# A chunked delta rule: the state updates of two heads as one full-height matmul, from values spread over zero-padded tiles

## The chip, the core and the metric

The kernel runs on one core of a Trainium2 chip. The core has a matrix engine (TensorE, called PE in profiles; its weight loads are listed apart as PEld), a vector engine (VectorE, DVE), an activation engine (ScalarE, ACT), GpSimd (POOL) and a queue that mostly issues transfers (SyncE, SP). Data lies in SBUF, matmul results in the eight banks of PSUM, the rest in HBM. Both on-chip memories have 128 partitions; "height" below is the number of partitions that an instruction works on. The metric is the device time of one execution in microseconds, the median of several runs.

## What is computed

One step of a two-layer streaming encoder for 2048 new frames of one stream and 32 frames of a running one, in fp32. The first layer is sliding-window attention, the second a gated delta rule with 8 heads, keys and values 128 wide, in chunks of 64 frames. The change lies in the second. Its recurrence, cut to what matters:

```python
def step(s, xs):                      # one chunk of 64 frames, all heads
    qi, ki, ui, wi, gi, ai = xs
    v_new = ui - einsum('bhcd,bhde->bhce', wi, s)
    o = einsum('bhcd,bhde->bhce', qi * exp(gi)[..., None], s) + einsum('bhij,bhje->bhie', ai, v_new)
    g_last = gi[..., -1]
    s = s * exp(g_last)[..., None, None] + einsum(
        'bhcd,bhce->bhde', ki * exp(g_last[..., None] - gi)[..., None], v_new)
    return s, o
```

The state `s` is 128x128 for each head. The last line is the state update that the change touches: for each head the transposed, weighted keys (64 frames x 128) times the new values (64 frames x 128).

## The kernel before

The 2048 frames run in four slabs of 512 (the second carries the 32 frames of the other stream too). For each slab the first layer's projections and attention are done, all four slabs first, then the second layer slab by slab. A slab of the second layer has 33 input blocks, each a product of 1024x128 weights with the slab (24 matmuls into a bank `pj`, each 512 or 272 columns wide, in a reduced fp32 format `fp32r`, high and low parts apart), and 8 output blocks. Beside these blocks run generators ("sides"): convolution, gates, the inverse of the chunk's triangular matrix, and the chain that walks through the chunks.

Heads go in pairs. The 64 frames of a chunk for the first head of the pair lie on partitions 0 to 63, those of the second on 64 to 127, so that one 128-partition tile holds both. Four chunks form a quad, and `chain_quad` (from line 1617) walks through its four chunks in order, since each needs the state left by the one before. There are 33 quads (4 slabs x 4 pairs x 2, and one for the other stream), so 132 steps. Quads of index 0 and 1 have buffers of their own, so that a quad of one pair can run beside a quad of the next pair. One step is:

1. two matmuls of keys and queries (`kq`) with the two heads' states (`st`), into a PSUM bank `tb` (p1);
2. `r` on DVE (two instructions of 64 partitions) and `qs` on ACT (two of 64), from p1;
3. a matmul of the inverse (`tt`, in profiles `btt`) with `r`, into a second bank `tb` (p2): the new values of both heads, one below the other;
4. an ACT copy of them into `vn`, 128x128;
5. the state updates: for each head the 64 rows of `kd` (weighted keys) as weights, and the 64 rows of `vn`, give a 128x128 product. The first head's goes to the bank `tc` (p3), the second's to a free quarter of p2, because two such matmuls on different halves of the rows go to different banks;
6. a matmul of `it` (in profiles `bit`, the masked products of queries and keys) with `vn`, into p2;
7. on DVE one instruction for each head, state = state x decay + product (`st<-st,egl,tc` and `st<-st,egl,tb`), and the sum `o`;
8. on ACT the squares of `o`.

The program is written once by generators and then sorted: `Order` (line 211) keeps all recorded operations with their dependencies, and `flush` places them engine by engine with the planner's costs (`Estimate.cost`, line 119), the operations of a step ahead of others (`lead = Order.CHAIN`). A PSUM bank counts as a whole in these dependencies: a DVE read of p2 is placed after every PE write to p2 that was recorded before it. Each engine then runs its list in order. For PE, the planner's cost of a 128x128 fp32 matmul and its cost of one 128x256 wide are nearly in the ratio 1 to 2.

All the instructions issued through this layer bear line 185 in the profile, so the tiles' names tell them apart: `tc<-vn,kd` and `tb<-vn,kd` are the two updates, `tb<-vn,bit` the matmul of point 6.

Of the kernel before, what the change touches and what calls it, by code (L numbers as in the profile page):

```python
# [16 lines left out]
P = 128  # L17
# [5 lines left out]
CH = 64  # L23
# [359 lines left out]
class Kern:  # L383
# [846 lines left out]
    def delta_setup(self, bp):  # L1230
        nc = self.nc
        self.bp = bp
        one = lambda shape, tag, dt=F32: self.t(bp, shape, tag, dt, bufs=1)
        self.st = one([P, DNH, P], "st")
        self.hist = one([P, 24, 3], "hist")
        nc.gpsimd.memset(self.hist, 0.0)
        self.hsmp = one([P, 24, 3], "hsmp")
        nc.sync.dma_start(self.hsmp, self.io["cv"])
        self.csmp = one([P, 24, 3], "csmp")

        self.cw = one([P, 96], "cw")
        nc.vector.tensor_scalar(out=self.cw, in0=self.par[:, PC_CW : PC_CW + 96], scalar1=0.5, scalar2=None, op0=ALU.mult)
        self.dg = one([P, 1], "dgn")
        nc.vector.tensor_scalar(out=self.dg, in0=self.par[:, PC_DG : PC_DG + 1], scalar1=0.5, scalar2=None, op0=ALU.mult)
        self.na_ = one([P, 4], "na")
        nc.scalar.activation(self.na_, self.par[:, PC_AL : PC_AL + 4], AF.Exp)
        nc.vector.tensor_scalar(out=self.na_, in0=self.na_, scalar1=-1.0, scalar2=None, op0=ALU.mult)

        self.tts = [one([P, 4, P], f"btt{i}") for i in range(2)]
        self.its = [one([P, 4, P], f"bit{i}") for i in range(4)]  # L1250

        def zeros():
            for x in (*self.its, *self.tts, self.st):
                nc.gpsimd.memset(x, 0.0)
                yield 1000

        self.spawn(zeros(), "zeros", 5000)
        self.npair = self.nconv = 0
        self.chained, self.order, self.quads, self.had = set(), [], [], [None, None]
# [357 lines left out]
    def chain_quad(self, q, tab, off, states, gated, put):  # L1617


        nc, bp, m = self.nc, self.bp, 4  # L1620
        tt = nc.vector.tensor_tensor
        kq = q["kq"]
        yield from self.take(f"chain{q['i']}")
        yield from self.take("o", 2)
        o = self.t(bp, [P, 4, P], "o", bufs=2)
        so = self.t(bp, [P, 4], "so", bufs=2)
        al = q["al"]
        for c in range(m):
            state = yield from states(c)
            p1 = yield from self.bank("tb")  # L1630
            self.issue.lead = Order.CHAIN
            for x in range(2):
                self.mm(p1[:, x * P : (x + 1) * P], kq[:, c, x, :], state[:, x, :], True, True)
            r = self.t(bp, [P, P], f"r{q['i']}", bufs=1)
            qs = self.t(bp, [P, P], f"qs{q['i']}", bufs=1)
            half = [slice(y * CH, (y + 1) * CH) for y in range(2)]
            for x, rows in enumerate(half):
                nc.vector.scalar_tensor_tensor(
                    out=r[rows], in0=p1[rows, x * P : (x + 1) * P], scalar=q["nbk"][rows, c : c + 1], in1=q["vb"][rows, c, :],
                    op0=ALU.mult, op1=ALU.add)  # L1640
            for x, rows in enumerate(half[::-1]):
                nc.scalar.activation(
                    qs[rows], p1[rows, x * P : (x + 1) * P], AF.Identity, scale=tab["egq"][rows, off + c : off + c + 1])
            self.give("tb")
            self.issue.lead = 0
            yield
            p2 = yield from self.bank("tb")
            self.issue.lead = Order.CHAIN
            self.mm(p2[:, 0:P], q["tt"][:, c, :], r, True, True)
            vn = self.t(bp, [P, P], f"vn{q['i']}", bufs=1)  # L1650
            nc.scalar.copy(vn, p2[:, 0:P])
            self.issue.lead = 0
            yield

            p3 = yield from self.bank("tc")
            up = [p3[:, 0:P], p2[:, 2 * P : 3 * P]]
            self.issue.lead = Order.CHAIN
            for x in range(2):
                rows = slice(x * CH, (x + 1) * CH)
                self.mm(up[x], q["kd"][rows, c, :], vn[rows], True, True)  # L1660
            self.mm(p2[:, P : 2 * P], q["it"][:, c, :], vn, True, True)
            for x in range(2):
                nc.vector.scalar_tensor_tensor(
                    out=state[:, x, :], in0=state[:, x, :], scalar=tab["egl"][:, x, off + c : off + c + 1],
                    in1=up[x], op0=ALU.mult, op1=ALU.add)
            tt(out=o[:, c, :], in0=p2[:, P : 2 * P], in1=qs, op=ALU.add)
            self.issue.lead = 0
            self.give("tb")
            self.give("tc")
            yield  # L1670
            nc.scalar.activation(qs, o[:, c, :], AF.Square, accum_out=so[:, c : c + 1])
            states.done(c)

        q["over"].append("kq")
        self.give(f"chain{q['i']}")

        def rest():

            yield so
            tt(out=so[:, :m], in0=so[:, :m], in1=al, op=ALU.mult)  # L1680
            tt(out=so[:, :m], in0=so[:, :m], in1=al, op=ALU.mult)
            nc.vector.tensor_scalar(out=so[:, :m], in0=so[:, :m], scalar1=1.0 / P, scalar2=EPS, op0=ALU.mult, op1=ALU.add)
            nc.gpsimd.tensor_tensor(out=so[:, :m], in0=so[:, :m], in1=self.mhalf[:, :m], op=ALU.pow)
            yield
            tt(out=so[:, :m], in0=so[:, :m], in1=al, op=ALU.mult)
            yield
            for c in range(m):
                nc.scalar.activation(o[:, c, :], o[:, c, :], AF.Copy, scale=so[:, c : c + 1])
            yield
            po = yield from self.bank("ta")  # L1690
            for c in range(m):
                self.tp(po[:, c * P : (c + 1) * P], o[:, c, :])
            yield
            while not gated():
                yield 100
            zs = q["zs"]
            yield zs
            w = zs.shape[3]
            tt(out=zs, in0=po.rearrange("p (c x t) -> p c x t", x=2, t=CH)[:, :, :, :w], in1=zs, op=ALU.mult)
            self.give("ta")  # L1700
            self.give("o")
            yield
            yield from put(zs)
            q["over"].append("zs")

        return rest()
# [528 lines left out]
```

## Time and profile before

| | us |
|---|---|
| median of 3 runs | 2395.19 |
| lowest and highest | 2393.38, 2398.52 |
| the profiled execution | 2401.5 |
| its span, first to last instruction | 2399.7 |
| second layer in the span, from about | 1030 |

The mean granted TensorE clock of the profiled execution is 0.971 of full speed. In a profile's row of a group stand the line, the engine, the operation, the tiles (out<-in), the shape, the count, then busy time in us, the mean length of one in ns, and the idle time of the engine just before, with what ended it. Rows of the timeline begin with the start in us and the length; equal neighbours are merged, with their count at the end. A fp32 matmul of the program stands as two MATMUL records and two LDWEIGHTS records, so 132 matmuls count 264.

### The profile page before, as it was taken

What the parts mean: (1) busy time and instruction counts of PE and PEld (TensorE: products, weight loads), DVE (VectorE), ACT (ScalarE), POOL (GpSimd) and SP (SyncE); (2) the same over time, 40 slices, a digit from 0 to 9 for tenths busy, and PEclk for the clock granted to TensorE, in tenths of its full rate; (3) what the DMA queues carried; (4) which work ended last, traced back from release to release, by engine and by line L of the source; (5) the groups of instructions that cost most, each with busy time, mean ns of one, the idle gap of its engine ahead of it and who ended that gap; (6) DMA issues with size and microseconds to landing.
All of it is one profiled execution on the core that took longest, in us unless ns stands there. A gap on an engine that the chain in (4) does not pass through costs nothing.

```text
span 2399.7 us, 44456 instructions
## 1 busy us (share of the span) xinstructions
PE 2279.1 (95%) x14759; PEld 1851.9 (77%) x14759; DVE 1644.0 (69%) x5024; ACT 1265.6 (53%) x3792; POOL 864.4 (36%) x1044
## 2 busy tenths in 40 slices
PE   8999999899999999999999999999999999999997
PEld 5667888797778777777779798876798777777776
DVE  6765465726562546488888768888786888886876
ACT  5555465636553555355666454674554466445533
POOL 4566555565554333223322122331312222222222
PEclk9998999999999999999999999998999989999998
DMA  7565755476525124644334564334456634466541
GB/s 253 167 190 181 240 181 177 150 252 213 176 89 164 63 64 135 199 159 139 121 109 133 181 226 154 120 99 136 138 162 213 213 113 139 138 212 214 159 141 67
DMA packets 222832, 382.75 MB, mean 159 GB/s; under 512 B 29922, under 2 KB 45194, under 8 KB 222602
## 3 DMA queue, kind: packets, MB, share of 16 engines
q1 hardware_dynamic: 220154, 377.75, 49.4%
q8 instruction: 116, 1.90, 0.3%
q10 hardware_dynamic: 2448, 2.16, 0.3%
q14 instruction: 114, 0.93, 0.1%
HBM read 311.63 MB, written 68.19 MB: 158 GB/s over the span
## 4 chain that ended last, share of the span: by engine, by line
PE 57%; DVE 24%; ACT 7%; issue 3%; DMA 3%; POOL 2%; SPq 0%; DVEq 0%; ACTq 0%; POOLq 0%
PE pj L185 41%; PE tb L185 6%; PE ta L185 5%; PE tc L185 4%; DVE cy L185 3%; DVE s L185 3%; DVE sub L185 2%; DVE tl L185 2%; ACT s L185 1%; DVE ml L185 1%; ACT ta L185 1%; DVE r L185 1%; DVE mx L185 1%; DVE md L185 1%; DVE xa L185 1%
## 5 line engine op out<-in xcount | busy, mean ns | idle before, releaser
L185 PE MATMUL pj<-hk,wh 128*128 128x512 f32 (+1 forms) x8184 | 1796.7, 365 | 23.1 <-DVE xr L185 6.8
L185 PEld LDWEIGHTS pj<-hk,wh 128*128 128x128 f32 x8184 | 1331.4, 192 | 237.2 <-issue 22.9
L185 POOL TENSOR_TENSOR wh<-wr,wh 128x512 fp32r<-128x512 f32 x224 | 295.3, 1321 | 333.2 <-ACT wh L185 282.0
L185 DVE SCALAR_TENSOR_TENSOR cy<-cx,cw,cy 128x512 f32<-128x512 f32 x360 | 230.8, 651 | 45.0 <-ACT cy L185 40.3
L185 ACT CAST wh<-wr 128x512 fp32r<-128x512 f32 x224 | 137.7, 617 | 215.3 <-PE pj L185 164.3
L185 ACT ACTIVATE s<-s,mx 128x256 f32<-128x256 f32 (+1 forms) x272 | 132.0, 487 | 32.3 <-DVE mx L185 32.0
L185 ACT ACTIVATE qs<-tb,egq 64x128 f32<-64x128 f32 x264 | 95.8, 363 | 88.4 <-DVE r L185 76.0
L185 DVE TENSOR_SCALAR s<-s,den 128x256 f32<-128x256 f32 (+1 forms) x272 | 133.6, 542 | 1.3
L185 DVE TENSOR_TENSOR sub<-ml,tl 128x60 f32<-128x60 f32 (+24 forms) x527 | 126.5, 240 | 10.2
L185 ACT ACTIVATE cx<-cy 128x512 f32<-128x512 f32 (+1 forms) x96 | 61.1, 636 | 130.9 <-DVE cy L185 104.4
L185 DVE TENSOR_TENSOR tl<-tl,sub 128x60 f32<-128x60 f32 (+24 forms) x527 | 122.8, 233 | 10.0
L185 POOL TENSOR_TENSOR pr<-pr,ph 128x512 fp32r<-128x512 f32 x82 | 111.2, 1356 | 40.6 <-ACT ph L185 37.7
L185 DVE CUSTOM_DVE_ANT_0 s<-ta,bias 128x256 f32<-128x256 f32 (+1 forms) x272 | 96.3, 405 | 39.3 <-PE ta L185 38.0
L185 POOL COPY cx<-hist 128x3 f32<-128x3 f32 x96 | 26.7, 278 | 264.3 <-DVE kq L185 62.7
L185 DVE TENSOR_TENSOR xr<-pj,xr 128x512 f32<-128x512 f32 (+1 forms) x72 | 41.2, 577 | 108.3 <-PE pj L185 72.1
L185 POOL TENSOR_TENSOR so<-so,mhalf 128x4 f32<-128x4 f32 x33 | 36.8, 1114 | 218.0 <-DVE so L185 190.2
L185 DVE SCALAR_TENSOR_TENSOR r<-tb,nbk,vb 64x128 f32<-64x128 f32 x264 | 91.8, 348 | 29.9 <-PE tb L185 25.3
L185 ACT ACTIVATE qs<-o 128x128 f32<-128x128 f32 x132 | 40.7, 308 | 133.4 <-DVE o L185 128.1
L185 ACT COPY cx<-pj 128x512 f32<-128x512 f32 (+2 forms) x149 | 64.1, 446 | 78.9 <-PE pj L185 63.5
L185 PE MATMUL tc<-pt,vt 128*64 128x128 f32 (+2 forms) x1056 | 91.3, 289 | 12.1 <-ACT pt L185 11.3
L185 PE MATMUL tb<-st,kq 128*128 128x128 f32 x512 | 95.7, 289 | 6.4 <-DVE st L185 5.7
L185 PEld LDWEIGHTS tb<-st,kq 128*128 128x128 f32 x512 | 83.4, 196 | 21.3 <-DVE st L185 13.1
(242 smaller groups left out, 3578.6 us busy)
## 6 DMA issues: line engine op xcount, KB each, us to landing
wh<-xswwd SPq DMA_DIRECT2D x528, 256.0 KB, 2.9
wr<-in_wa SPq DMA_DIRECT2D x160, 256.0 KB, 2.9
wh<-xswwdo SPq DMA_DIRECT2D x112, 256.0 KB, 2.9
pr<-in_wd SPq DMA_DIRECT2D x66, 256.0 KB, 4.0
xswwd<-ph SPq DMA_DIRECT2D x66, 256.0 KB, 2.7
xswwd<-pr SPq DMA_DIRECT2D x66, 256.0 KB, 3.6
wr<-in_wao SPq DMA_DIRECT2D x64, 256.0 KB, 2.9
xa<-in_x SPq DMA_DIRECT2D x48, 256.0 KB, 3.3
```

The costliest lines, as they stand in the source:

```text
L185: self.order.add(Op(self.name, lambda: call(*args, **kw), cost, op == "dma_start"), ins, outs)
```

## The change

The new values are copied three times instead of once. Two copies of 64 partitions put the first head's values into the left half of a new tile `vz` (128 partitions x 2 x 128 values) and the second head's into its right half; the other rows of each half are zero, cleared once by GpSimd at the start of the layer. There are two such tiles, one for each quad index. Then one matmul with all 128 rows of `kd` as weights and all 256 columns of `vz` gives both heads' products, side by side in p3: the zero rows keep the heads apart. The third copy, of full height, fills `vn` as before, for the matmul with `it`. The quarter of p2 that held the second product is not used any more.

```diff
         self.its = [one([P, 4, P], f"bit{i}") for i in range(4)]
+        self.vz = [one([P, 2, P], f"vz{i}") for i in range(2)]
 
         def zeros():
-            for x in (*self.its, *self.tts, self.st):
+            for x in (*self.its, *self.vz, *self.tts, self.st):
                 nc.gpsimd.memset(x, 0.0)
                 yield 1000
...
             vn = self.t(bp, [P, P], f"vn{q['i']}", bufs=1)
+            vz = self.vz[q["i"]]
+            for x, rows in enumerate(half):
+                nc.scalar.copy(vz[rows, x, :], p2[rows, 0:P])
             nc.scalar.copy(vn, p2[:, 0:P])
...
             p3 = yield from self.bank("tc")
-            up = [p3[:, 0:P], p2[:, 2 * P : 3 * P]]
+            up = [p3[:, x * P : (x + 1) * P] for x in range(2)]
             self.issue.lead = Order.CHAIN
-            for x in range(2):
-                rows = slice(x * CH, (x + 1) * CH)
-                self.mm(up[x], q["kd"][rows, c, :], vn[rows], True, True)
+            self.mm(p3[:, 0 : 2 * P], q["kd"][:, c, :], vz.rearrange("p x d -> p (x d)"), True, True)
             self.mm(p2[:, P : 2 * P], q["it"][:, c, :], vn, True, True)
```

Since the planner sorts all operations, the order changes on every engine from the first step on. The places below are one step in the first slab of the second layer, beside its output blocks. `pj` rows are matmuls of an output block, the number behind a name is its buffer.

PE before, from the matmul with the inverse to the next step's first matmuls:

```order
L185 MATMUL tb_12189<-r_3195_12185,btt_2199_11189 128x128
L185 MATMUL pj_12221<-hk_11503,wh_12197 128x512 x2
L185 MATMUL pj_12221<-hk_11503,wh_12198 128x512
L185 MATMUL tc_12191<-vn_3200_12190,kd_12046 128x128
L185 MATMUL tb_12189<-vn_3200_12190,kd_12046 128x128
L185 MATMUL tb_12189<-vn_3200_12190,bit_2201_11191 128x128
L185 MATMUL pj_12221<-hk_11504,wh_12197 128x512 x2
L185 MATMUL tb_12192<-st_11182,kq_11959 128x128
L185 MATMUL pj_12221<-hk_11504,wh_12198 128x512
L185 MATMUL pj_12221<-hk_11692,wh_12197 128x512 x2
L185 MATMUL tb_12192<-st_11182,kq_11959 128x128
```

PE after, the same place:

```order
L185 MATMUL tb_12199<-r_3207_12197,btt_2199_11189 128x128
L185 MATMUL pj_12205<-hk_11513,wh_12186 128x512 x2
L185 MATMUL pj_12205<-hk_11513,wh_12187 128x512
L185 MATMUL pj_12205<-hk_11514,wh_12186 128x512
L185 MATMUL tc_12201<-vz_2205_11195,kd_12029 128x256
L185 MATMUL tb_12199<-vn_3210_12200,bit_2201_11191 128x128
L185 MATMUL pj_12205<-hk_11514,wh_12186 128x512
L185 MATMUL pj_12205<-hk_11514,wh_12187 128x512
L185 MATMUL pj_12205<-hk_11697,wh_12186 128x512 x2
L185 MATMUL pj_12205<-hk_11697,wh_12187 128x512
L185 MATMUL tb_12206<-st_11182,kq_11953 128x128 x2
```

The update is one matmul in place of two and stands one `pj` later; the next step's two `st,kq` matmuls stand together, five `pj` behind `bit`, where they stood apart, two and five behind it.

ACT, before:

```order
L185 ACTIVATE qs_3196_12186<-tb_12184,egq_11946 64x128 x2
L185 COPY vn_3200_12190<-tb_12189 128x128
L185 ACTIVATE sq_12223<-xr_12180 128x512
L185 ACTIVATE qs_3196_12186,so_12172<-o_12171 128x128
L185 ACTIVATE qs_3204_12194<-tb_12192,egq_11946 64x128 x2
```

and after:

```order
L185 ACTIVATE qs_3208_12198<-tb_12196,egq_11941 64x128 x2
L185 COPY vz_2205_11195<-tb_12199 64x128 x2
L185 COPY vn_3210_12200<-tb_12199 128x128
L185 ACTIVATE sq_12209<-xr_12168 128x512
L185 ACTIVATE qs_3208_12198,so_12182<-o_12181 128x128
```

The two half copies come first, the full copy behind them, and the rest of the list keeps its order.

DVE, the state updates, before:

```order
L185 TENSOR_TENSOR xr_12180<-pj_12200,xr_12180 128x512
L185 SCALAR_TENSOR_TENSOR st_11182<-st_11182,egl_11947,tc_12191 128x128
L185 TENSOR_TENSOR acc_12152<-acc_12152,sq_12223 128x512
L185 SCALAR_TENSOR_TENSOR st_11182<-st_11182,egl_11947,tb_12189 128x128
L185 TENSOR_TENSOR o_12171<-tb_12189,qs_3196_12186 128x128
```

and after:

```order
L185 TENSOR_TENSOR xr_12168<-pj_12189,xr_12168 128x512
L185 TENSOR_TENSOR acc_12162<-acc_12162,sq_12209 128x512
L185 SCALAR_TENSOR_TENSOR st_11182<-st_11182,egl_11942,tc_12201 128x128 x2
L185 TENSOR_TENSOR o_12181<-tb_12199,qs_3208_12198 128x128
```

Both updates read `tc` and stand together; the sum `acc` of an output block moves ahead of them.

## The prediction

> **What bounds the kernel now.** I read the page's head and its table of engines first, then the busy time by stage, then single instructions.
>
> ```profile
> span 2399.7 us, 44456 instructions
> PE 2279.1 (95%) x14759; PEld 1851.9 (77%) x14759; DVE 1644.0 (69%) x5024; ACT 1265.6 (53%) x3792; POOL 864.4 (36%) x1044
> ...
> PE 57%; DVE 24%; ACT 7%; issue 3%; DMA 3%; POOL 2%; SPq 0%; DVEq 0%; ACTq 0%; POOLq 0%
> ```
>
> TensorE (PE) carries the span: 95% busy and 57% of the chain that ended last. The view of busy time by stage splits off the second layer, in which the change lies; its columns are PE, PEld, DVE, ACT, POOL, each with its instructions, then the granted clock, the DMA share and GB/s.
>
> ```profile
> 0.00:1030.00 1030.00, 979.55 (x6161) 782.76 (x6163) 556.80 (x1606) 546.30 (x1435) 515.00 (x460) 0.98 0.53 170
> 1030.00:1345.00 315.00, 303.00 (x2061) 249.85 (x2057) 266.79 (x864) 183.00 (x601) 93.75 (x161) 0.99 0.42 132
> 1345.00:1610.00 265.00, 250.96 (x1966) 225.31 (x1964) 204.15 (x649) 138.95 (x486) 67.29 (x138) 0.98 0.51 162
> 1610.00:2400.00 790.00, 745.57 (x4579) 594.02 (x4579) 616.28 (x1908) 397.34 (x1272) 188.31 (x287) 0.95 0.50 156
> ```
>
> From 1030 us to the end (1370 us) PE is busy 1299.5 us (95%), DVE 1087.2 (79%), ACT 719.3 (53%). So the stage with the 132 chain steps is bound by PE, with DVE not far behind and ACT half free. What a step costs on PE is the first question, what it makes other engines wait for the second.
>
> **What a step costs on PE today.** Each fp32 matmul stands in the trace as two passes, each with a weight load. The groups by shape, from 1030 us on:
>
> ```profile
> L185 PE MATMUL tb<-st,kq 128*128 128x128 f32 x512 | 95.7, 289 | 6.4 <-DVE st L185 5.7
> L185 PE MATMUL tb<-vn,bit 128*128 128x128 f32 x264 | 65.9, 332 | 0.0
> L185 PE MATMUL tc<-vn,kd 64*128 64x128 f32 x264 | 65.6, 329 | 3.2 <-ACT vn L185 2.7
> L185 PE MATMUL tb<-vn,kd 64*128 64x128 f32 x264 | 65.6, 329 | 0.0
> L185 PE MATMUL tb<-r,btt 128*128 128x128 f32 x248 | 51.8, 291 | 12.8 <-DVE r L185 11.9 <-DVE btt L185 0.4
> ```
>
> The half-height pair and the `bit` matmul behind it take longer per pass (329 and 332 ns) than other 128x128 matmuls (289, 291). Durations overlap, so the price is read from starts. One step, on PE alone, where the work around it is regular (start, length, instruction, count):
>
> ```profile
> 1369.91 0.38 PE L185 MATMUL tb<-r,btt 128*128 128x128 f32 x2
> 1370.05 0.93 PE L185 MATMUL pj<-hk,wh 128*128 128x512 f32 x3
> 1370.91 0.37 PE L185 MATMUL tc<-vn,kd 64*128 64x128 f32 x1
> 1370.92 0.37 PE L185 MATMUL tb<-vn,kd 64*128 64x128 f32 x1
> 1371.13 0.27 PE L185 MATMUL tc<-vn,kd 64*128 64x128 f32 x1
> 1371.13 0.27 PE L185 MATMUL tb<-vn,kd 64*128 64x128 f32 x1
> 1371.34 0.49 PE L185 MATMUL tb<-vn,bit 128*128 128x128 f32 x2
> 1371.58 0.70 PE L185 MATMUL pj<-hk,wh 128*128 128x512 f32 x2
> 1372.12 0.38 PE L185 MATMUL tb<-st,kq 128*128 128x128 f32 x2
> 1372.26 0.94 PE L185 MATMUL pj<-hk,wh 128*128 128x512 f32 x3
> 1373.04 0.38 PE L185 MATMUL tb<-st,kq 128*128 128x128 f32 x2
> 1373.18 1.40 PE L185 MATMUL pj<-hk,wh 128*128 128x512 f32 x5
> 1374.42 0.38 PE L185 MATMUL tb<-r,btt 128*128 128x128 f32 x2
> ```
>
> - From 1372.12 to 1373.04 (0.92 us) stand one 128x128 matmul and 3 `pj`; from 1373.04 to 1374.42 (1.38) one and 5 `pj`. So a `pj` takes 0.23, and an ordinary 128x128 matmul 0.92 - 0.69 = 0.23, 0.11 or 0.12 a pass.
> - From 1369.91 to 1370.91 (1.00) stand one such matmul and 3 `pj`, 0.92; 0.08 is left, lost ahead of the pair.
> - From 1370.91 to 1372.12 (1.21) stand the pair, `bit` and 2 `pj` (0.46). Pair and `bit` take 0.75; with the loss ahead of them, **0.83**.
>
> The pair's members start together, yet its passes are 0.21 apart, twice an ordinary pass, and `bit` takes what is left. The weight loads show why:
>
> ```profile
> 1370.91 0.18 PEld L185 LDWEIGHTS tc<-vn,kd 64*128 64x128 f32 x1 [0.36 <-ACT vn L185]
> ...
> 1371.33 0.30 PEld L185 LDWEIGHTS tb<-vn,bit 128*128 128x128 f32 x2
> ```
>
> They start with the matmuls they serve instead of ahead of them. I read this as a change of the array's shape that lets no load run ahead, on the way in and on the way out.
>
> **What the new step costs on PE.** It has one full-height matmul of 256 columns and `bit`. No fp32 matmul of 256 columns runs at full clock in this trace; the nearest from both sides are the 128 columns above (0.11 a pass) and this one of 512:
>
> ```profile
> 25.86 1.02 PE L185 MATMUL ms<-rb,ones 128*128 128x512 f32 x2
> ...
> L185 PE MATMUL ms<-rb,ones 128*128 128x512 f32 x2 | 1.0, 592 | 0.0
> ```
>
> Its two passes end 1.02 us after the first start and last 0.59 each: 0.43 apart. A pass of 256 columns lies between 0.11 and 0.43; I take half of 0.43, 0.21, since 128 columns take a quarter. The new step is 2 x 0.21 + 0.23 = **0.66**, and 0.83 - 0.66 = 0.17 us goes from each of 132 steps: 22 us. But the new matmul's first load can hide only if its operand is there while the work ahead still runs. Today's load waited for the copy in some of the steps:
>
> ```profile
>   PEld tc L185: 24.6, 62
> ```
>
> (from the view of the tile `vn`: who waited for it, us and times). If in those 62 a load of 0.11 stays exposed, 62 x 0.11 = 7 us comes back: between 15 and 22 us of PE time goes, 19 as the middle.
>
> Here the Trainium skill has a rule against the change. "TensorEngine Tiling (Array Packing)", section Key Properties, says that tiles operate independently and different tiles load and multiply in parallel. By that alone the pair would cost one matmul, 0.23, and the new one 0.43: 132 x 0.20 = 26 us more. The trace has the parallel start (1370.91 and 1370.92), but not the price: the pair's passes are 0.21 apart.
>
> **What ACT gets.** 264 copies of 64x128 join the 132 of 128x128, ahead of them. That half the height saves nothing is seen on copies of equal width:
>
> ```profile
> L185 ACT COPY cx<-pj 128x512 f32<-128x512 f32 x66 | 38.3, 580 | 34.9 <-PE pj L185 28.4 <-DVE kq L185 4.7 <-DVE vf L185 1.5
> L185 ACT COPY kd<-ta 64x512 f32<-64x512 f32 x62 | 34.9, 578 | 6.3 <-PE ta L185 5.5
> ...
> 1506.71 0.25 ACT L185 COPY vn<-tb 128x128 f32<-128x128 f32 x1
> 1506.86 0.43 ACT L185 COPY cx<-pj 128x240 f32<-128x240 f32 x2
> ```
>
> A copy of 128 columns lasts 0.25 and lets the next begin after 0.15. So ACT gets 264 x 0.15 = 40 us on 719 of 1370. I cost its time at nothing because ACT stands idle for 47% of the stage. If that cover is gone, each step holds back for 0.3 us what is queued behind the copies on ACT, the `cx` and `cy` copies that empty the `pj` banks.
>
> **What the chain of a step gets.** The new matmul waits for the second copy, 0.15 after the one it waits for now. Today's DVE rows in the step above:
>
> ```profile
> 1371.44 0.35 DVE L185 SCALAR_TENSOR_TENSOR st<-st,egl,tc 128x128 f32<-128x128 f32 x1 [0.63 <-PE tc L185]
> 1371.70 0.68 DVE L185 TENSOR_TENSOR acc<-acc,sq 128x512 f32<-128x512 f32 x1
> 1372.30 0.34 DVE L185 SCALAR_TENSOR_TENSOR st<-st,egl,tb 128x128 f32<-128x128 f32 x1
> ```
>
> The first state update starts 0.53 after the pair. Tomorrow the second pass starts 0.21 after the first and lasts 0.59 - 0.21 = 0.38; with the 0.05 that DVE takes to follow (1371.44 less 1371.13 + 0.27), 0.64. With the copy's 0.15 and without the 0.08 ahead of the pair, the first update is 0.18 late. The second one today reads the bank that `bit` writes: it cannot start before 1371.34 + 0.49 + 0.05 = 1371.88, 0.97 after the pair. Tomorrow it follows the first after 0.26: 0.90 + 0.15 - 0.08 = 0.97, the same. Where DVE was given other work between the two, as here, it was 1.39, and the wait goes. So the chain from step to step is level at its tightest and up to 0.4 shorter elsewhere. I count it as nothing, with ends of +0.18 (if the first update decides) and -0.4.
>
> `bit` and the output sum wait for the third copy, 0.3 later than now; `bit` is queued behind 0.43 of the new matmul, which covers that. The two new clears on POOL are of a known size (128x256, 312 ns in the trace) and lie in the first layer's last part, where POOL is half idle. DMAs keep their number; the shifted order moves weight loads on the SP queue by a few rows, for which I allow 5 us either way.
>
> **The sum.** 19 us of PE time goes. Not all of it arrives: DVE, at 79%, then becomes what PE waits for more often. I choose three quarters, between nothing and all: 14 us. The profiled execution took 2401.5 us (span 2399.7), 6.3 above the median of 2395.2; less 14 it would be 2387.5, and against the median the forecast is **2381**, by itself 2372 to 2389.
>
> **The rivals.**
> - *All of it arrives, and the freed second update helps as well.* 22 us, and of 132 x 0.4 = 53 us of shortened chain perhaps a tenth: 2368. For it: PE's 95%. Against: PE already stands before `st` and `r` (6.4 and 12.8 us above).
> - *Absorbed.* The passes get shorter and PE waits for DVE's updates at the same clock time: 2390 to 2400. For it: DVE at 85% from 1030 to 1345 us (266.79 of 315). That the full-height step keeps two of its loads exposed gives the same answer: 0.66 + 2 x 0.11 = 0.88, level with today's 0.83 within the reading of these rows.
> - *Slower, through the first update.* If the chain of steps rather than PE sets the pace, each step is 0.18 later at the first update: 132 x 0.18 = 24 us where the steps stand in one row, half where two heads' chains overlap: 2407 to 2419. It decides from the point at which PE regularly stands before `st` or `r`. Against: these waits are 19 us of 1370 now.
> - *Slower, through the loads.* If full-height loads did not overlap, each of four passes would pay 0.11: 0.66 + 0.44 = 1.10 against 0.83, 132 x 0.27 = 36 us: 2431. Against: the 0.11 pitch of the `st,kq` passes, whose loads run under other matmuls. The Trainium skill states such a rule ("TensorE: Matmul & The Clock Gate", section Part 3: loads overlap with running matmuls only when the row group differs); by that rule this rival holds, and the trace speaks against it.
>
> **How the numbers follow.** Forecast 0.50, all arrives 0.15, absorbed 0.18, slower through the first update 0.14, through the loads 0.03. About 0.2% (5 us) is what a measurement of this kernel can tell from no change. Faster by more than that: 0.48 + 0.15 + 0.02 = 0.65; within it: 0.19; slower: 0.16. The range takes in the rival in which all arrives, the absorbed case and the near edge of the first slower one: 2363 to 2403, with some 0.2 left outside.
>
> **What would show it.** In the changed profile: a group of 264 passes, 128x256, full height, 0.21 apart, with no 0.08 ahead; `bit`'s passes 0.11 apart; `vz` copies of 0.25, 0.15 apart; both state updates back to back on DVE. The forecast is wrong if the new passes are over 0.3 apart, if PE's idle time before `st` and `r` grows by more than 10 us, or if the step saves its 0.17 and the span doesn't move.

## The result, and the profile after

The changed kernel takes 2405.33 us (median of 11 runs, 2399.16 to 2412.72), the kernel before 2395.19 (11 runs beside it): a ratio of 1.0035, with an interval of 1.0019 to 1.0052. It is slower by 10 us, where 14 us faster were forecast, and just above the range's end of 2403. The profiled execution took 2408.59 us.

The head of the page of the changed kernel:

```profile
span 2406.8 us, 44136 instructions
PE 2265.8 (94%) x14495; PEld 1862.1 (77%) x14495; DVE 1633.1 (68%) x5024; ACT 1332.6 (55%) x4056; POOL 869.8 (36%) x1046
...
PE 53%; DVE 27%; ACT 9%; issue 3%; DMA 2%; POOL 2%; SPq 0%; DVEq 0%; ACTq 0%; POOLq 0%
```

PE is busy 13.3 us less than before (2279.1), the span is 7.1 us longer, and ACT is busy 67.0 us more (1265.6 before). In the chain that ended last PE falls from 57% to 53%, DVE and ACT rise.

The step on PE, in the timeline (start, length, instruction, count) and in the groups by shape:

```profile
1374.97 0.38 PE L185 MATMUL tb<-r,btt 128*128 128x128 f32 x2
1375.11 1.16 PE L185 MATMUL pj<-hk,wh 128*128 128x512 f32 x4
1376.10 0.65 PE L185 MATMUL tc<-vz,kd 128*128 128x256 f32 x2
1376.59 0.38 PE L185 MATMUL tb<-vn,bit 128*128 128x128 f32 x2
1376.73 1.40 PE L185 MATMUL pj<-hk,wh 128*128 128x512 f32 x5
1377.98 0.63 PE L185 MATMUL tb<-st,kq 128*128 128x128 f32 x4
```

```profile
L185 PE MATMUL tb<-st,kq 128*128 128x128 f32 x512 | 86.0, 288 | 5.7 <-DVE st L185 4.5 <-ACT qs L185 0.7
L185 PE MATMUL tc<-vz,kd 128*128 128x256 f32 x264 | 85.9, 407 | 7.5 <-ACT vz L185 7.2
L185 PE MATMUL tb<-vn,bit 128*128 128x128 f32 x264 | 51.6, 278 | 0.0
```

`bit` passes last 278 ns where they lasted 332, and start 0.11 apart where it was 0.21 (medians). From 1376.59 to 1377.98 (1.39) stand `bit` and 5 `pj` of 0.23, so `bit` costs 0.24 in all. It starts 0.49 behind the update here; over all steps the median is 0.24 between the two wide passes and 0.215 from the second to `bit`. TensorE's part of the step is 0.69 by these medians, close to what the prediction said. The 0.24 between the wide passes is a mixture: 0.215 in 64 steps, and about 0.32 in most of the 56 above 0.28, in which the first weight load starts right behind the copy; the mean is 0.27. The loss ahead is gone: behind a 512-wide `pj` the update starts 0.23 later (median), where it was 0.33.

The same step on ACT, first of the kernel before (rows that the prediction does not show), then after:

```profile
1374.29 0.74 ACT L185 ACTIVATE qs<-tb,egq 64x128 f32<-64x128 f32 x2 [0.95 <-DVE r L185]
1374.93 0.25 ACT L185 COPY vn<-tb 128x128 f32<-128x128 f32 x1
```

```profile
1374.85 0.74 ACT L185 ACTIVATE qs<-tb,egq 64x128 f32<-64x128 f32 x2 [0.95 <-DVE r L185]
1375.49 0.52 ACT L185 COPY vz<-tb 64x128 f32<-64x128 f32 x2
1376.03 0.27 ACT L185 COPY vn<-tb 128x128 f32<-128x128 f32 x1
1376.19 0.63 ACT L185 ACTIVATE sq<-xr 128x512 f32<-128x512 f32 x1
```

The two half copies take 0.52 and hold `vn` back by 0.54 (1376.03 less 1375.49); behind the full-height `vn` the next begins after 0.16. The two half-height copies do not run into one another as the full-height ones in the prediction do. The kernel before already had such a pair: two `qs` of 64 rows take 0.74, twice their mean of 363 ns.

Where the time comes back shows in one stretch, the end of the second slab. Busy times from 1640 to 1840 us, before and after (columns as in the prediction):

```profile
1640.00:1840.00 200.00, 197.07 (x1400) 165.48 (x1399) 157.66 (x528) 104.83 (x351) 45.11 (x72) 0.97 0.50 156
```

```profile
1640.00:1840.00 200.00, 185.76 (x1230) 160.91 (x1229) 148.80 (x502) 109.48 (x373) 44.97 (x70) 0.94 0.46 147
```

PE is idle 14.2 us there against 2.9. Up to about 1650 us the changed kernel is ahead: pass 6000 of the 8184 `pj` passes starts at 1645.7 us, before at 1662.8. Pass 6300 starts at 1761.5 against 1753.9. The timeline of PE after, within:

```profile
1736.15 0.61 PE L185 MATMUL tb<-sst,kqs 128*128 128x128 f32 x4
1740.60 0.49 PE L185 MATMUL tb<-r,btt 128*128 128x128 f32 x2 [3.84 <-DVE r L185]
...
1748.04 1.35 PE L185 MATMUL ta<-con,o 128*128 128x128 f32 x4 [3.26 <-ACT o L185]
1750.87 1.11 PE L185 MATMUL ta<-con,vf 128*128 128x128 f32 x4 [1.48 <-DVE zss L185]
```

The projections had run ahead of the chain, so the chain of the quad of the other stream (`sst,kqs`, called the sample quad below) stands with little beside it, and PE waits. That is a reading of one stretch; the first experiments test it.

### The profile page after: what moved, and what is told of

Same layout as the page of the kernel before. It is cut to its first block, busy times and chain, and to the rows that moved or that the text cites. A ratio compares the mean times of both kernels' runs of the same rounds, so it can differ in the third digit from the quotient of the medians.

```text
span 2406.8 us, 44136 instructions
## 1 busy us (share of the span) xinstructions
PE 2265.8 (94%) x14495; PEld 1862.1 (77%) x14495; DVE 1633.1 (68%) x5024; ACT 1332.6 (55%) x4056; POOL 869.8 (36%) x1046
## 4 chain that ended last, share of the span: by engine, by line
PE 53%; DVE 27%; ACT 9%; issue 3%; DMA 2%; POOL 2%; SPq 0%; DVEq 0%; ACTq 0%; POOLq 0%
PE pj L185 38%; PE ta L185 5%; PE tb L185 5%; PE tc L185 5%; DVE cy L185 4%; DVE s L185 3%; DVE sub L185 2%; DVE tl L185 2%; ACT s L185 2%; DVE ml L185 1%; ACT ta L185 1%; DVE mx L185 1%; DVE r L185 1%; DVE md L185 1%; DVE st L185 1%
## 5 line engine op out<-in xcount | busy, mean ns | idle before, releaser
L185 DVE SCALAR_TENSOR_TENSOR st<-st,egl,tc 128x128 f32<-128x128 f32 x256 | 77.3, 343 | 75.4 <-PE tc L185 73.1
L185 PE MATMUL tb<-con,s 128*128 128x128 f32 (+2 forms) x528 | 84.6, 281 | 15.5 <-DVE s L185 10.6
L185 PEld LDWEIGHTS tc<-pt,vt 128*64 128x64 f32 (+1 forms) x1056 | 61.8, 139 | 45.6 <-ACT pt L185 25.7
```

The costliest lines, as they stand in the source:

```text
L185: self.order.add(Op(self.name, lambda: call(*args, **kw), cost, op == "dma_start"), ins, outs)
```

## The experiments

Eighteen kernels ran. All ratios are to the kernel before, run beside them on the same chip, with their 95% intervals. Two questions came first: is the loss that stretch (the theory called A in the expectations), or the copies, wherever they stand? The first four kernels are sorted anew by the planner, like the changed kernel.

**Sample quad in the old form.** The changed kernel, but the four steps of that quad keep copy and pair as before.

```diff
+            wide = not q.get("sample")
+            if wide:
                 for x, rows in enumerate(half):
                     nc.scalar.copy(vz[rows, x, :], p2[rows, 0:P])
```

> The changed kernel, but the one quad of the 32 frames (4 of the 132 steps) keeps the pair of half-height matmuls and the single copy. Theory A (the step gains on PE as forecast, and the loss is one hole at the end of the second slab, where PE waits in its order for this quad's steps; between two matmuls of the projections the changed kernel goes there from 21 us ahead to 8 us behind): the hole goes, 2378 to 2390. Theory B (each step's chain is longer by its two copies, and that costs everywhere): 4 steps of 132 change nothing, 2400 to 2408. Theory C (any new sorting of the instructions moves the time by some us, whatever it does): anything from 2390 to 2410.

0.9981 [0.9966, 0.9997], 2392.19 us. Four steps out of 132 in another form, and the time moved by 13 us. That is more than four steps hold: something else moved, the order. Nor did the stretch go: PE is still idle 11.0 us between 1640 and 1840 us, after 14.2 in the changed kernel.

**Copies alone.** The kernel before, with the two half copies ahead of `vn`; nobody reads them.

```diff
             vn = self.t(bp, [P, P], f"vn{q['i']}", bufs=1)
+            vz = self.vz[q["i"]]
+            for x, rows in enumerate(half):
+                nc.scalar.copy(vz[rows, x, :], p2[rows, 0:P])
             nc.scalar.copy(vn, p2[:, 0:P])
```

> The kernel before with the two half copies added ahead of the full copy; nobody reads their tiles, and the pair of half-height matmuls stays. Theory A: the copies lie in ACT's idle time, 2393 to 2402. Theory B: the copies alone cost what the change cost and what it gained on PE, 8 + 15 to 22 us: 2410 to 2425. Theory C: as for any new sorting, within 10 us of 2395.

1.0046 [1.0031, 1.0062], 2408.58 us. The copies alone reproduce the loss, and the running ahead too: `pj` pass 6000 starts at 1645.0 us, pass 7200 at 2027.6 (before 2016.8). So that was no gift of the shorter matmul; the order with the copies in it makes it. What the matmul adds (1.0035 against 1.0046) the two intervals do not separate. The time lies between the ranges of theories B and C.

**Zeros in the weights.** The keys' scaling on ACT, which exists already, writes into padded tiles ahead of the step; two full-height matmuls of 128 columns, one copy.

```diff
+                nc.scalar.activation(kz[rows, x, :], q["kd"][rows, c, :], AF.Copy, scale=q["kds"][rows, c : c + 1])
...
-                self.mm(up[x], q["kd"][rows, c, :], vn[rows], True, True)
+                self.mm(up[x], kz[:, x, :], vn, True, True)
```

> The kernel before with two full-height matmuls of 128 columns in place of the half-height pair; the zeros stand in the weights (the keys, scaled into padded tiles ahead of the step in place of the scaling that the kernel does anyway), so that the step has one copy of the values as before. PE has the same two passes of 256 columns in all (4 of 128, 0.43 us). Theory A: the gain on PE of 15 to 22 us arrives unless a hole opens again: 2375 to 2385, or near 2400 with a hole. Theory B: without the copies in the chain the gain on PE arrives: 2373 to 2385. Theory C: 2380 to 2400.

0.9988 [0.9973, 1.0003], 2395.23 us: level. No half copy stands in the chain of a step, but ACT's busy time is 1325.7 us, 60 more than before.

**A nudged planner, after and before.** The planner's delay from ACT to PE is raised from 270 to 285 ns; not an instruction changes but the order does. First in the changed kernel, later, as a control, in the kernel before.

```diff
-        "scalar": {"tensor": 270, "vector": 145, "scalar": 34, "gpsimd": 160},
+        "scalar": {"tensor": 285, "vector": 145, "scalar": 34, "gpsimd": 160},
```

> The changed kernel with the planner's lag from ACT to PE at 285 instead of 270 ns: the same instructions, sorted a little differently. Theory A: the hole depends on the sorting at one place, so it may go: 2385 to 2405. Theory B: the same instructions cost the same, 2402 to 2409. Theory C: over 4 us away from 2405, either way.

> The kernel before with the planner's lag from ACT to PE at 285 instead of 270 ns, as in the nudged changed kernel (which went from 1.0035 to 1.0005): the same instructions, sorted a little differently. Theory C (a new sorting moves the time by some us by itself): 4 us or more away from 2395. Otherwise within 3 us of it.

The changed kernel: 1.0005 [0.9991, 1.0020], 2400.37 us. The kernel before: 0.9983 [0.9970, 0.9997], 2395.32 us. So sorting the same instructions anew moves the time by 4 to 7 us, as much as what was to be explained; the 4 us of the control are small, with an interval that ends at 0.9997. In the nudged changed kernel `pj` pass 6000 is 24.6 us ahead and pass 6300 1.3: it has theory A's stretch too, and yet is level. A as the one cause falls.

From here the order had to be held. The next kernels keep the order of the kernel before on every engine and issue the extra instructions right beside the one they belong to.

**Copies in the old order, ahead of `vn` or behind it.** Unread half copies from p2.

```diff
+            self.beside_last(*[(nc.scalar.engine.copy, vz[rows, x, :], p2[rows, 0:P]) for x, rows in enumerate(half)], ahead=True)
```

> The two half copies ahead of the full copy, nobody reads them, and every engine keeps the order of the kernel before (the copies are issued with the full copy and the planner does not see them). The copies with a new sorting took 1.0046 of the time before. Theory D (that was the new sorting, the copies themselves lie in idle time): 2393 to 2399. Theory B (the copies delay the step in fact): 2403 to 2410.

> As the copies ahead, but behind the full copy, so that ACT has the same work and the step's values come as early as before. Theory B, by the delay of the step: 2393 to 2399, while the copies ahead take 2403 to 2410. If it is ACT's time rather than the delay: both the same, 2403 to 2410. Theory D: both 2393 to 2399.

Ahead: 1.0160 [1.0147, 1.0173], 2434.43 us; behind: 1.0152 [1.0136, 1.0168], 2432.56 us. In a held order the copies cost 36 to 38 us, some four times the loss of the changed kernel, and over 20 us above every range that was expected. The group of the first update, copies ahead:

```profile
L185 PE MATMUL tc<-vn,kd 64*128 64x128 f32 x264 | 65.6, 329 | 34.1 <-ACT vn L185 33.0
```

What DVE sat idle for before its state updates (view of the tile `st`, us and times), before and with the copies ahead:

```profile
  PE tc L185: 57.4, 50
```

```profile
  PE tc L185: 81.6, 73
```

PE waits 33.0 us for `vn` where it waited 2.7, and DVE in turn for the update. Copies behind `vn` do not delay it, but they read the PSUM bank into which the second matmul of the pair writes; a bank counts as a whole in the dependencies, so that matmul waits for them instead. One step of that run:

```profile
1379.96 0.54 ACT L463 COPY vz<-tb 64x128 f32<-64x128 f32 x2
```

```profile
1380.30 0.49 PE L185 MATMUL tc<-vn,kd 64*128 64x128 f32 x2
1380.54 0.48 PE L185 MATMUL tb<-vn,kd 64*128 64x128 f32 x2
```

The copies end at 1380.50 and the second matmul starts at 1380.54, 0.24 behind the first, where the two start together in the kernel before. Over the 132 steps the time from the pair's start to what follows `bit` on PE grows from 95.6 to 122.2 us.

**Where ACT's time stands, without that wait.** Three unread variants in the old order: half copies behind `vn`, reading `vn` and not PSUM; two full-height copies ahead of `vn`; and, of the zeros in the weights (sorted anew), one with the scaling on POOL.

```diff
+            self.beside_last(*[(nc.scalar.engine.copy, vz[rows, x, :], vn[rows]) for x, rows in enumerate(half)], ahead=False)
```

```diff
+            self.beside_last(*[(nc.scalar.engine.copy, vz[:, x, :], p2[:, 0:P]) for x, rows in enumerate(half)], ahead=True)
```

```diff
-                nc.scalar.activation(kz[rows, x, :], q["kd"][rows, c, :], AF.Copy, scale=q["kds"][rows, c : c + 1])
+                nc.gpsimd.tensor_tensor(
+                    out=kz[rows, x, :], in0=q["kd"][rows, c, :], in1=q["kds"][rows, c : c + 1].broadcast_to([CH, P]), op=ALU.mult)
```

> The copies behind the full copy, in the order of the kernel before, but they read vn and not the PSUM bank, so that PE's writes to that bank (the second of the pair, and bit) do not wait for them. ACT's work is that of the other two copies' runs (1.016 and 1.0152 of before); the step's values come as early as before, to all who read them. Theory B (the delay of the step, which PE waits out before the pair): 2394 to 2404. Theory E (ACT's own time, whatever waits): 2425 to 2436.

> The two copies ahead of vn, in the order of the kernel before, but each of full height (128x128 instead of 64x128; nobody reads them). In the run with half-height copies each held ACT for 0.27 us, since it did not overlap with its neighbour, and vn came 0.54 late; 38 us over 132 steps is 0.29 a step, so some 0.25 of a delay lies in the order's slack. If full copies follow each other after 0.15, as vn and its follower do in the kernel before, vn is 0.3 late and most of it is slack: 2396 to 2408. If two more copies cost the same whatever their height: 2428 to 2438.

> The padded keys, but scaled into their tiles by POOL instead of ACT, which has 132 scalings less: the step has one copy, PE the full-height matmuls, ACT some 38 us less, POOL some 264 instructions of 64x128 more (100 us or so, in a stage where it is busy 25%). If the step's gain on PE arrives by half, as in the run with full-height matmuls in the old order (0.9954), and nothing waits for POOL: 2376 to 2388. If the lighter ACT counts too: 2365 to 2376. If the steps wait for POOL's scalings: over 2400.

Behind, from `vn`: 1.0118 [1.0100, 1.0137], 2427.62 us. Groups of PE in it:

```profile
L185 PE MATMUL tb<-st,kq 128*128 128x128 f32 x512 | 97.8, 292 | 11.8 <-DVE st L185 10.5 <-ACT qs L185 0.5
L185 PE MATMUL tc<-vn,kd 64*128 64x128 f32 x264 | 65.6, 329 | 3.5 <-ACT vn L185 3.1
L185 PE MATMUL tb<-r,btt 128*128 128x128 f32 x248 | 53.0, 296 | 16.3 <-DVE r L185 15.6 <-DVE btt L185 0.4
```

The pair waits no more (3.1 us, before 2.7), and still 28 us are lost: PE waits longer for `st` (10.5, before 5.7) and `r` (15.6, before 11.9). ACT's time costs through what is queued behind it, as what DVE waits for shows (us in total, times, longest), before and in this run:

```profile
DVE cy L185 <- ACT cy L185: 33.1, 23, 2.9
DVE ss L185 <- ACT ta L185: 18.1, 24, 2.0
```

```profile
DVE cy L185 <- ACT cy L185: 42.3, 28, 3.1
DVE ss L185 <- ACT ta L185: 31.0, 33, 2.8
```

These are rows of the convolution and of the keys' norms, work that prepares later steps.

Two full-height copies: 1.0071 [1.0051, 1.0090], 2415.40 us. They carry twice the rows of the half copies and cost less than half, a time between the two ranges expected. ACT in it:

```profile
1377.94 0.41 ACT L463 COPY vz<-tb 128x128 f32<-128x128 f32 x2
1378.24 0.26 ACT L185 COPY vn<-tb 128x128 f32<-128x128 f32 x1
```

Both hold `vn` back by 0.30 where the half copies do by 0.54. That is the rate that the prediction had taken, and at this rate the copies would have cost 17 us in this order.

Scaling on POOL: 1.0135 [1.0116, 1.0154], 2429.94 us. POOL's busy time rises from 864.4 to 984.2 us, and POOL stands 239.3 us before these scalings until PE has read the tile's earlier contents. So moving the work to a third engine did not help, but how much of the loss is its own stays open: the granted clock of these four runs is 0.964 to 0.970, that of the kernel before beside them 0.976 in the mean, and among those runs 0.01 of clock goes with 13 us. By that estimate some 12 of the 32 us are the clock's.

**The whole change in the old order, and the matmul alone.** The first keeps the order of before but for some ten rows, with wide matmul and copies. The second leaves the copies out: both matmuls of the pair take all 128 rows of `kd` and `vn`, so that the two heads' updates are summed into both states; so what is computed differs, and PE runs two full-height matmuls of 128 columns in place of the half-height pair.

```diff
+                    self.issue.ops[-1].call = lambda w=wide, p3=p3: nc.tensor.engine.matmul(p3[:, 0 : 2 * P], *w, start=True, stop=True)
```

```diff
-                self.mm(up[x], q["kd"][rows, c, :], vn[rows], True, True)
+                self.mm(up[x], q["kd"][:, c, :], vn, True, True)
```

> All of the change's instructions in the order of the kernel before, but for some ten rows; the new matmul stands at the first of the pair. Theory D: the forecast's gain arrives, 2375 to 2387. Theory B: the copies' 11 us less the 3 us of the matmul, 2400 to 2406. A third one, that both halves of the story are the sorting's: 2392 to 2398.

> The kernel before, in its own order on every engine, with both matmuls of the pair on all 128 rows (the two heads' updates are summed, so the states are not the reference's): no copy is added, and PE loses the 0.17 us a step. If PE sets the pace as the forecast said: 2371 to 2381. If the gain is absorbed by what PE waits for, as the padded keys' 0.9988 suggests: 2388 to 2396.

The whole change: 1.0085 [1.0072, 1.0098], 2417.22 us, above all three ranges. Full height alone: 0.9954 [0.9938, 0.9970], 2382.52 us. The step on PE with full height alone:

```profile
1360.52 0.38 PE L185 MATMUL tc<-vn,kd 128*128 128x128 f32 x2
1360.74 0.39 PE L185 MATMUL tb<-vn,kd 128*128 128x128 f32 x2
1360.96 0.39 PE L185 MATMUL tb<-vn,bit 128*128 128x128 f32 x2
```

```profile
L185 PE MATMUL tb<-st,kq 128*128 128x128 f32 x512 | 94.4, 285 | 10.6 <-DVE st L185 10.1 <-ACT qs L185 0.4
```

Each matmul costs 0.22, the step 0.66 as predicted for the wide one, so 22 us of PE time are gone. Of these 11 arrive (0.46%). Of the rest 4.4 are seen at once: PE waits 10.1 us for `st`, before 5.7. As much goes before the matmuls of the triangular inverse, which wait 9.1 us for DVE's `tq`, before 4.8.

**More work for PE.** The counter-test: the old order with one more matmul of 128 columns in each step, its result unread.

```diff
+            op.call = lambda f=op.call, out=p2[:, 3 * P : 4 * P], a=q["it"][:, c, :], v=vn: (
+                f(), nc.tensor.engine.matmul(out, a, v, start=True, stop=True))
```

> The kernel before in its own order, with one more matmul of 128 columns per step, its result unread: PE gets about 0.22 us x 132 = 29 us. If PE's time counts by half, as the shorter step of the run with full-height pairs did: 2408 to 2415 us. If it counts fully, since PE is the bound: 2422 to 2430. If PE's waits take it in: 2395 to 2402.

1.0070 [1.0050, 1.0089], 2413.83 us.

```profile
L185 PE MATMUL tb<-st,kq 128*128 128x128 f32 x512 | 93.1, 283 | 4.5 <-DVE st L185 4.0
L1664 PE MATMUL tb<-vn,bit 128*128 128x128 f32 x264 | 52.0, 279 | 0.0
```

Some 30 us (132 x 0.23) are added and 17 arrive: again a little over half, and now PE waits less for `st`. A microsecond of PE time counts half here in both directions, though PE is "95% busy".

**The price the planner has for a copy.** The planner's formula makes a half copy 158 ns; the trace says 0.26 to 0.28 from start to start. In the changed kernel the price is raised to 270; in the next the copies carry the keys' scale (and the 132 scalings on ACT go); the third does both.

```diff
+        if engine == "scalar" and out.tensor.name.startswith("vz"):
+            return 270.0
```

```diff
-                nc.scalar.copy(vz[rows, x, :], p2[rows, 0:P])
+                nc.scalar.activation(vz[rows, x, :], p2[rows, 0:P], AF.Copy, scale=q["kds"][rows, c : c + 1])
```

> The changed kernel, with the planner's price of each half-height copy raised from 158 to 270 ns; instructions as in the changed kernel, sorted anew. If the copies cost because the planner thought them cheap and packed PE's order too tight behind them: 2393 to 2400 us. If ACT's time itself is what costs, or the pair comes later whatever the order: 2401 to 2408. Sorting anew alone has moved the time by 4 to 7 us, so a difference below that decides nothing.

> The changed kernel, but the two copies multiply by the key's scale on their way, and the 132 scalings of the keys on ACT (about 0.29 us each, 38 us) go. If ACT's time counts where it stands in the step: 2388 to 2398 us. If only the delay of the pair behind the copies counts, which stays: 2400 to 2408.

> The former with the copies' price raised to 270 ns as well. If price and ACT's time both count: 2383 to 2393 us, faster than both kernels. If only one does: as the better of the two alone, 2390 to 2400. If neither: 2400 to 2408.

Price alone: 0.9973 [0.9959, 0.9988], 2390.89 us, **faster than both kernels**. Scaled copies: 1.0016 [1.0003, 1.0029], 2402.10 us; both: 0.9992 [0.9979, 1.0004], 2394.30 us. The second test missed its aim, as the view of its tile `vz` shows:

```profile
L185 ACT ACTIVATE vz<-tb,kds x264: 346/363/383, 1067.9 to 2371.0; 64x128 f32<-64x128 f32 x132
```

With a scale from a tile a half copy lasts 363 ns instead of 260 (medians), and ACT is busy 1326.0 us, only 6.6 less than in the changed kernel. The end of the second slab at the price of 270:

```profile
1640.00:1840.00 200.00, 195.14 (x1335) 168.82 (x1335) 153.19 (x524) 117.17 (x390) 49.80 (x77) 0.98 0.51 161
```

PE is idle 4.9 us there instead of 14.2: the stretch is gone. It does not tell the time, though: with the scaled copies PE is idle 3.2 us there, in a kernel slower than before, and in the faster sample-quad run 11.0. Two more prices were to tell whether 270 was a lucky sorting.

> The changed kernel with the planner's price of a half-height copy at 240 ns in place of 158 (the run before had 270 and 2391 us). If an honest price is what helps: 2388 to 2398 us. If 270 was a lucky sorting: anywhere from 2391 to 2407, as the sortings so far lay.

> The same with 300 ns. If an honest price is what helps: 2388 to 2398 us, as with 240. If 270 was a lucky sorting: anywhere from 2391 to 2407, and the two not alike.

At 240: 0.9996 [0.9978, 1.0014], 2396.85 us. At 300: 1.0003 [0.9991, 1.0015], 2397.07 us. Both are better than the changed kernel, both short of 270, and level with the kernel before. The best of the sortings is 2391 us, but the price does not promise it.

## Why the prediction was wrong, point by point

- **The step on PE: right.** Predicted 0.66 in place of 0.83; measured 0.69, and 0.66 in the run with full height alone. The 7 us allowed for exposed first loads came as well: 0.27 less 0.215 between the wide passes, times 132. Of the signs that were to show the forecast wrong, the last one came: the step saves its time and the span does not follow. The rival in which full-height loads don't overlap is refuted by these pitches (the passes of `bit` 0.11 apart); so is the rule of the Trainium skill named with it ("TensorE: Matmul & The Clock Gate", section Part 3), for these shapes.
- **"So ACT gets 264 x 0.15 = 40 us on 719 of 1370. I cost its time at nothing because ACT stands idle for 47% of the stage": the step that failed, twice.** The size was taken from full-height copies; half copies cost 67 us. The row that would have told it, the two `qs` in 0.74, is in the trace of before. And idle time elsewhere does not cover a copy that stands in the chain of a step: in a held order the copies cost 38 us ahead of `vn`, and 28 where the pair does not wait for them. By ACT's busy time beyond the 1265.6 us of before:

| old order | ACT us more | us slower |
|---|---|---|
| half copies ahead of `vn` | 65.6 | 38 |
| half copies behind, from `vn` | 82.7 | 28 |
| full-height copies ahead | 40.9 | 17 |

(us slower is the ratio less 1, times 2397.) A third to over half of each microsecond given to an engine 53% busy arrived at the end. Copies behind `vn` that read PSUM stay out of the table, since there PE's own wait for the bank is most of the loss.
- **"I choose three quarters": too much.** In the old order half arrives, 11 of 22 us, and half of an addition too. Busy shares are made of modelled ends, and 95% did not mean that the stage is PE's alone; most of the other half is seen in longer waits for DVE, which is near the "absorbed" rival, but only 4.4 us of it stand before the state updates that this rival named.
- **The chain counted as nothing, with the first update 0.18 later.** Counted from the start of the matmul with the inverse (medians over all steps), the update's matmul went from 1.24 to 1.48 us, DVE's first state update from 1.99 to 2.46 and the end of the second from 2.83 to 3.06. So the first is 0.47 late and the second 0.23, outside the ends of +0.18 and -0.4: the second half copy ends later than assumed, and the planner put `pj` matmuls and DVE's `acc` ahead. Yet a longer step alone does not make the loss: at the price of 270 the second update ends at 3.28, in the fastest kernel of the change. The rival "slower through the first update" gave 2407 to 2419 and came nearest to the time, but its mechanism was not the one alone: with no wait of the pair, 28 us were still lost behind the copies on ACT.
- **The order allowed 5 us either way.** That was about right for one sorting (4 and 7 us in the two nudged kernels), but five sortings of the changed instructions lie from 0.9973 to 1.0035, 15 us apart.

Put together, in the old order the change is -11 (matmul) and +38 (copies ahead of `vn`), +27; the whole change measured +20 there. Its matmul waits for the second half copy and not for `vn` behind it: it starts 1.30 us after the matmul with the inverse (median), the pair behind the unread copies 1.57. The planner, which sorts with the copies in view, takes back most of this: 1.0035, and 0.9973 to 1.0005 in the four other sortings, 1.0002 in their mean with it. So the change is worth nothing within some 0.3%, and where in that spread it lands is the sorting. That the planner's price of 158 ns is to blame is possible but not settled: the three higher prices gave 0.9973, 0.9996 and 1.0003, the low price 1.0005 and 1.0035, and the worst of the three is as good as the better of the two.

## What to carry to other kernels

Price an added instruction at the place where it stands, by the nearest row of the same height on the same engine: one that delays what a serial chain waits for, or what is queued behind it, costs part of its time however idle the engine is on average. A bound engine's saving should be tested both ways, by taking time away and by adding some, before it is counted in full. Where a planner sorts the program, hold the order for the experiment and nudge the planner for a control, or the sorting will be taken for the effect.

## What the runs showed of the hardware

- Two copies of 64 partitions on different halves did not overlap on ACT: 0.26 from start to start, and 0.28 to the full-height one behind them, where full-height copies follow after 0.15. It is not the height alone: the second `qs`, also of 64 partitions, is 363 ns long, and a copy behind it starts after 0.265. Two full-height copies are quicker than two of half the height (0.30 against 0.54 us until `vn` starts). The Trainium skill ("ScalarE: Activation LUTs", section What ACT_TABLE_LOAD costs) states that ACTIVATE instructions back to back overlap by about 93 ns; the full-height copies agree (0.25 long, 0.15 apart), the pair of `qs` (363 ns long, 375 apart) and the half-height copies do not. Why was not tried.
- A pair of half-height fp32 matmuls that start together costs as much as two full-height ones in a row (0.42 and 0.45 from the first start to `bit`, medians), and the change of height takes 0.17 more in a step (0.83 against 0.66): 0.33 against 0.23 from the 512-wide `pj` ahead of it, 0.24 against 0.14 from `bit` to what follows.
